# Half of the low weight parts made by an accumulating DMA

## The chip, the cores and the metric

The kernel runs on one core of a Trainium2 chip. The metric is the device time of one execution in microseconds (us).

## The reference

A trunk of two layers over 256 tokens with 2048 features, all in float32. Each of its four sub-layers ends in `x <- LayerNorm(ALPHA * x + sublayer(x))`.

```
layer 0: z = gelu(x @ w_in); u, v = split(z)                # 2048 -> 2 x 6144
         s = per-group 128 x 128 spatial weights (masked) on LayerNorm(v), + b_s
         (u * s) @ w_out                                    # 6144 -> 2048
layer 1: latent attention: q and kv latents of 512, 16 heads, rotary key of 64,
         chunk-causal softmax, output projection            # 2048 -> 2048
both:    h = causal width-3 depthwise conv(x @ w_up)        # 2048 -> 2 x 5504
         (silu(g) * a) @ w_down                             # 5504 -> 2048
```

With 256 tokens the weights are by far the largest data: every weight is read once and used for 256 tokens.

## The kernel before

**Float32 products in three parts.** A float32 value is written as the sum of a high part (rounded to the format that TensorE multiplies in one pass, `F32R` in the code) and a low part (value minus high part). A product is made of three: high x high, high x low and low x high. Activations are split as they arise. Weights are split chunk by chunk as they come from HBM.

**The chunks.** All weights are cut into 442 chunks of at most 128 x 2048 float32 (1 MB), numbered in the order of their use. 0 to 47 belong to stage `v`, 48 to 95 to stage `u`, 96 to 143 to `wo`, 144 to 229 to the up-projection of layer 0 (`up`), 230 to 272 to its down-projection (`dn`), 273 to 312 to the attention, 313 to 398 to the up-projection of layer 1, 399 to 441 to its down-projection.

**Feed.** The class `Feed` loads and splits them. `_load` takes a buffer `raw` and issues one plain DMA on SP's queue (L62). `_split` takes two more buffers, `wh` and `wl`, and for each half of the columns lets ACT copy the chunk into `wh`, which rounds it (L75), and DVE subtract `wh` from `raw` into `wl` (L76). `next(splits=2, loads=2)` hands out the next chunk, after it has put the splits of two chunks more, and the loads of two beyond those, into the streams. All of these buffers, together with the activations that live long, come from one pool of 22 buffers (`big`), so a load or a split waits until an earlier buffer is free.

**Order.** Each engine works through its own stream in order; the streams are laid down in about the order of the program, with splits moved ahead of evictions where the buffers allow it. ACT's stream thus mixes splits (L75) with evictions of finished products: in stage `u` and in the up-projection, `sum_halves` (L201 on ACT, L203 on DVE) and the convolution (L458 and following) for each group of four chunks. In these stages the weight is the stationary operand (`prod_a`): for every 128 x 128 block TensorE multiplies the high part with 512 columns (high and low part of the activation) and then the low part with 256 columns, so both parts of a chunk are needed within its first half microsecond. In the other stages the activation is stationary (`prod_b`), and each piece of 512 columns takes the high part twice and the low part once. All matmuls are issued by one helper and stand under L113.

**Layer boundaries.** `boundary` interleaves the last products of a sub-layer, its norm and the first products of the next one; there the splits of four chunks are asked for beforehand.

**GpSimd** sets a few constants at the start and one mask in stage `v` (L394), and issues no DMA.

Of the kernel before, what the change touches and what calls it, by code (L numbers as in the profile page):

```python
# [12 lines left out]
ALU = mybir.AluOpType  # L13
AX = mybir.AxisListType

P = 128
# [13 lines left out]
ALPHA = 4.0 ** 0.25  # L30
# [4 lines left out]

# columns of the per-partition constants
C_GMG = 0
# [5 lines left out]

# chunks at the end of a projection whose products are done block by block
SKEW = 3


class Feed:
    """The weight chunks in the order of their use: loaded ahead, and each split
    into a high and a low part whose sum is the float32 value."""  # L50

# [14 lines left out]
    def _split(self):  # L66
        i = self.split
        cols = self.chunks[i][1]
        raw = self.raw.pop(i)
        hi = self.pool.tile([P, 2048], F32R, tag="big", name=f"wh{i}")  # L70
        lo = self.pool.tile([P, 2048], F32R, tag="big", name=f"wl{i}")
        step = 512 if i == 0 else 1024 if cols == 2048 else cols // 2
        for o in range(0, cols, step):
            c = slice(o, o + step)
            self.nc.scalar.copy(hi[:, c], raw[:, c])  # L75
            self.nc.vector.tensor_tensor(lo[:, c], raw[:, c], hi[:, c].bitcast(F32), ALU.subtract)  # L76
        self.parts[i] = (hi, lo)
        self.split += 1
# [17 lines left out]
def trunk(ctx: ExitStack, tc: tile.TileContext, x, xT, gm_in, gm_wout, ffn_up, ffn_dn,  # L96
# [17 lines left out]

# [1 line left out]
    chunks = []  # L116
# [11 lines left out]

# [1 line left out]
    feed = Feed(nc, big, chunks)  # L130
    # products of zeros keep the array's clock up while the first loads are under way
    idle = cpool.tile([P, 512], BF16, name="idle")
# [5 lines left out]
    for j in range(4):  # L138
# [8 lines left out]
        for q in parts:  # L147
            hi = xhl[j][:, q, 0:S]
# [30 lines left out]

    # products whose stationary operand is the activation: [tokens, columns]  # L180
    def x_parts(xs, k, b):
# [3 lines left out]
    def prod_b(acc, parts, hi, lo, pieces, first, last):  # L185
        """acc: banks by piece; hi, lo: [P, columns]; pieces: (offset, width)"""
        xh, xl = parts
        for f, (o, w) in enumerate(pieces):
            mm(acc[f][:, :w], xh, hi[:, o : o + w], first, False)
            mm(acc[f][:, :w], xl, hi[:, o : o + w], False, False)  # L190
            mm(acc[f][:, :w], xh, lo[:, o : o + w], False, last)

    # products whose stationary operand is the weight: [features, 256 | 256]
    def prod_a(acc, xs, k, hi, lo, first, last):
# [11 lines left out]
    def split_act(src, name):  # L206
        """src: [P, 256] float32 -> high and low parts side by side"""
        t = tp.tile([P, 2 * S], F32R, tag="t2", name=name, bufs=6)
        nc.scalar.copy(t[:, 0:S], src)
        nc.vector.tensor_tensor(t[:, S : 2 * S], src, t[:, 0:S].bitcast(F32), ALU.subtract)  # L210
        return t
# [3 lines left out]
    def down(n_k, get_src, tag, ln, skew=SKEW):  # L215
        """[tokens, 2048] += src[k]^T w[k] with all eight banks; block 0 ends first"""
        acc = [[bank(f"{tag}_{b}_{f}") for f in range(4)] for b in range(2)]
        late = []
        a = {}
        for k in range(n_k):  # L220
            for j in range(k, min(k + 2, n_k)):
                if j not in a:
                    a[j] = split_act(get_src(j), f"{tag}a{j}")
            left = n_k - 1 - k
            hi, lo = feed.next(splits=2 if left > 8 else 3 if left > 3 else 4, loads=2 if left > 3 else 1)
            if left == 6:
                ln.prep()
            t = a.pop(k)
            if left < skew:
                late.append((t, hi, lo, k))  # L230
                continue
            for b in range(2):
                prod_b(acc[b], (t[:, b * P : (b + 1) * P], t[:, S + b * P : S + (b + 1) * P]),
                       hi, lo, full, k == 0, False)

        def end(b, f):
            for t, hi, lo, k in late:
                prod_b(acc[b][f : f + 1], (t[:, b * P : (b + 1) * P], t[:, S + b * P : S + (b + 1) * P]),
                       hi, lo, full[f : f + 1], False, k == n_k - 1)

        return acc, end

    def group(ln, tag):
        """the four chunks [4 k, 512 columns] after a norm, for block 0 and then for block 1"""
        parts = []
        acc = [bank(f"{tag}{b}") for b in range(2)]
        for b in range(2):
            for c in range(4):
                if b == 0:
                    parts.append(feed.next(splits=3 - c, loads=1))  # L250
                hi, lo = parts[c]
                for j in range(4):
                    k = 4 * c + j
                    prod_b([acc[b]], x_parts(ln.new, k, b), hi, lo, [(j * 512, 512)], k == 0, k == KD - 1)
                yield acc[b]

    def boundary(ln, acc, end, fs, tag, after):
        """the last products of a sub-layer, its norm, and the first products of the next one:
        each block's norm runs under the products of the other block"""
        for f in fs:  # L260
# [5 lines left out]
        if len(fs) == 2:  # L266
# [7 lines left out]
            g = group(ln, tag)  # L274
# [43 lines left out]
    class Norm:  # L318
        """LayerNorm(ALPHA * res + acc), in place of res; and its transpose in high and low parts"""

# [48 lines left out]

    # ================= layer 0: spatial-gating MLP =================  # L370
    halfp = [(0, 512), (512, 512)]
    v = []
    vst = st.tile([P, 2, 12, 6], F32, tag="vst", name="vst", bufs=1)
    for gi in range(6):
# [14 lines left out]
        if gi == 0:  # L389
            # spatial weights [j, g, i] with later chunks masked; sums over j and b_s on all partitions  # L390
            wT = slot([P, 2, 1024], "wT")
            wTg = wT[:, 0, :].rearrange("p (g i) -> p g i", g=NG)
            nc.sync.dma_start(wTg, w_sT)
            nc.gpsimd.memset(wTg[64:P, :, 0:64], 0.0)  # L394
            bsum = slot([P, 2, 1024], "bsum")
            nc.sync.dma_start(bsum[:, 1, :], b_s.to_broadcast([P, 1024]))
# [54 lines left out]

    # ================= gated MLP with the causal convolution =================
    def conv(layer, F, acc, name):
        """F: tile of the 86 up-projected feature tiles"""
        h = acc if acc.shape[-1] == S else sum_halves(acc, name)
# [56 lines left out]

    # ================= layer 1: latent attention =================
    cq = [slot([P, 4, 512], "cq", F32R)]
# [5 lines left out]
    def rope(dst, src, b, n, name):  # L520
        """dst, src: [P, n, 64]"""
        hf = ROPE // 2
# [11 lines left out]
    def latent(b, q, pieces):  # L534
        """RMS norm of a latent that lies in banks"""
        src = hqk[:, b, q * RANK : (q + 1) * RANK]
# [8 lines left out]
        o = 0  # L545
# [4 lines left out]
    def latent_put(b, q, dst, cg):  # L550
        """its transpose, in high and low parts"""
        src = hqk[:, b, q * RANK : (q + 1) * RANK]
# [47 lines left out]

    # rotary part of the queries: two chunks of [2 k, 1024]
    acc = [[bank(f"qr{b}_{f}") for f in range(2)] for b in range(2)]
# [20 lines left out]

    # head-major parts: four heads a chunk of [4 k, 512]
    def heads(dst, src, i, tag):
# [20 lines left out]
    def attend_a(h):  # L646
        """scores of head h and their softmax"""
        q, k = qT[h // 8][:, h % 8, :], kT[h // 8][:, h % 8, :]
# [5 lines left out]
        for b in range(2):  # L654
            nk = (b + 1) * P
            o = sc[:, cc[b]]
            # one accumulation bank for both blocks of queries
            mm(o, q[:, b * P : (b + 1) * P], k[:, :nk], b == 0, False)
            mm(o, qrT[r, h // 2, b * P : (b + 1) * P], krT[r, :nk], False, False)
            mm(o[:, nk - P : nk], negq, keyr, False, b == 1)  # L660
# [11 lines left out]
    def attend_b(h):  # L672
        """[keys of block 0, 256 queries | keys of block 1, 128 queries]"""
        p = probs[h]
# [34 lines left out]

    # output projection: two halves of the columns, the first one between the heads  # L710
    ln = Norm(2, res)
# [54 lines left out]
def _layout(inputs):  # L766
# [5 lines left out]
    def chunked(w, kk, width):  # L772
        """[K, N] -> [N / width * K / (128 kk), 128, kk * width]"""
        K, N = w.shape
        t = w.reshape(K // (P * kk), kk, P, N // width, width).transpose(3, 0, 2, 1, 4)
        return t.reshape(-1, P, kk * width)

    def pairs(w):
        """the up-projection: two tiles of a and two of g side by side"""
        n = (NF_FF // 2) * 2 * P  # L780
# [67 lines left out]
```

## Time and profile before

| | |
|---|---|
| time, median of 2 runs | 2565.43 us (2565.26 to 2565.59) |
| span of the profiled execution | 2564.7 us |
| TensorE matmuls | 2550.4 us busy, 99% |
| DVE | 1574.7 us, 61% |
| ACT | 1225.7 us, 48% |
| GpSimd | 2.4 us |
| DMA read from HBM | 476.00 MB, mean 186 GB/s over the span |

The profiled execution's span and the run times lie within a microsecond of each other, so durations of the trace can be set against the median directly. A row of a group or of the timeline names the line of the kernel, the engine, the operation and the tiles (output, arrow, inputs); in the timeline the first figure is the start, the second the duration, and the bracket at the end the idle time before it with what ended it. "PEclk" is the granted share of TensorE's full clock.

### The profile page before, as it was taken

The numbers are of one execution on the slowest core, as the hardware profiler recorded it, in microseconds if no ns is written. First come the engines' busy times: TensorE is split into PE (matmuls) and PEld (weight loads), VectorE is DVE, ScalarE is ACT, GpSimd is POOL, SyncE is SP. The second block draws the span as 40 slices with busy tenths as digits, with TensorE's granted clock in tenths as the row PEclk, the third lists the DMA queues.
The fourth block names the chain that finished last, engine by engine and source line by source line (L and its number), as shares of the span: only waits on it lengthen the run. The fifth ranks groups of instructions, "written<-read, shape, count | busy, mean of one in ns | idle before, by whom it ended". The sixth has DMA issues, their size and how long they took to land.

```text
span 2564.7 us, 32218 instructions
## 1 busy us (share of the span) xinstructions
PE 2550.4 (99%) x13041; PEld 2156.3 (84%) x13041; DVE 1574.7 (61%) x2284; ACT 1225.7 (48%) x1795; POOL 2.4 (0%) x15
## 2 busy tenths in 40 slices
PE   9999999999999999999999999999999999999998
PEld 7888888888888888888888888867888888888886
DVE  6444666675546766765675547745676576667554
ACT  6343444454443654654554434544365455446441
POOL 0000000000000000000000000000000000000000
PEclk9999999999999999999999999989999999999999
DMA  8555454466563645554565554423554454546552
GB/s 335 180 178 189 172 179 167 176 221 214 211 239 123 230 165 181 197 172 168 202 220 202 202 194 175 164 83 142 197 203 174 164 205 169 186 172 240 206 201 92
DMA packets 68837, 480.18 MB, mean 187 GB/s; under 512 B 7632, under 2 KB 8272, under 8 KB 11728
## 3 DMA queue, kind: packets, MB, share of 16 engines
q1 hardware_dynamic: 68688, 478.13, 52.1%
q8 instruction: 102, 1.67, 0.3%
q14 instruction: 47, 0.39, 0.0%
HBM read 476.00 MB, written 2.10 MB: 186 GB/s over the span
## 4 chain that ended last, share of the span: by engine, by line
PE 99%; DVE 1%; DMA 0%; SPq 0%; ACT 0%; issue 0%; DVEq 0%; ACTq 0%
PE up L113 36%; PE dn L113 18%; PE u L113 10%; PE wo L113 10%; PE v L113 10%; PE mo L113 4%; PE upf L113 2%; PE sc L113 2%; PE mkv L113 1%; PE qn L113 1%; PE kn L113 1%; PE vv L113 1%; PE mq L113 1%; PE s L113 1%; PE o L113 0%; PE qr L113 0%
## 5 line engine op out<-in xcount | busy, mean ns | idle before, releaser
L76 DVE TENSOR_TENSOR wl<-raw,wh 128x1024 fp32r<-128x1024 f32 (+2 forms) x886 | 1054.6, 1215 | 491.8 <-ACT wh L75 380.3
L75 ACT CAST wh<-raw 128x1024 fp32r<-128x1024 f32 (+2 forms) x886 | 890.7, 1044 | 567.7 <-DVE wl L76 242.0
L113 PE MATMUL up<-xhl,wh 128*128 128x512 f32 x2624 | 927.5, 399 | 0.0
L113 PE MATMUL up<-xhl,wl 128*128 128x256 f32 x2624 | 738.2, 281 | 0.0
L113 PEld LDWEIGHTS up<-xhl,wh 128*128 128x128 f32 x2624 | 493.8, 188 | 122.4
L113 PEld LDWEIGHTS up<-xhl,wl 128*128 128x128 f32 x2624 | 496.9, 189 | 0.1
L113 PE MATMUL u<-xhl,wh 128*128 128x512 f32 x768 | 268.8, 397 | 0.0
L113 PE MATMUL wo<-wh,woa 128*128 128x512 f32 x768 | 237.0, 390 | 0.0
L113 PE MATMUL v<-wh,xhl 128*128 128x512 f32 x768 | 235.5, 391 | 0.6 <-DVE xhl L150 0.3
L113 PE MATMUL u<-xhl,wl 128*128 128x256 f32 x768 | 212.5, 279 | 0.0
L113 PE MATMUL dn<-wh,dn0a 128*128 128x512 f32 x688 | 212.5, 390 | 0.0
L113 PE MATMUL dn<-wh,dn1a 128*128 128x512 f32 x688 | 211.8, 390 | 0.0
L113 PEld LDWEIGHTS v<-wh,xhl 128*128 128x128 f32 x768 | 144.2, 188 | 32.1 <-ACT wh L75 0.8
L113 PEld LDWEIGHTS u<-xhl,wh 128*128 128x128 f32 x768 | 143.5, 188 | 32.7
L113 PEld LDWEIGHTS wo<-wh,woa 128*128 128x128 f32 x768 | 144.1, 188 | 29.8
L113 PEld LDWEIGHTS dn<-wh,dn1a 128*128 128x128 f32 x688 | 129.2, 188 | 26.6
L113 PEld LDWEIGHTS dn<-wh,dn0a 128*128 128x128 f32 x688 | 129.1, 188 | 26.7
L113 PE MATMUL wo<-wl,woa 128*128 128x512 f32 x384 | 149.5, 390 | 0.0
L113 PE MATMUL v<-wl,xhl 128*128 128x512 f32 x384 | 147.3, 390 | 0.0
L113 PEld LDWEIGHTS u<-xhl,wl 128*128 128x128 f32 x768 | 144.8, 189 | 1.1
L113 PE MATMUL dn<-wl,dn0a 128*128 128x512 f32 x344 | 134.0, 390 | 0.0
L113 PE MATMUL dn<-wl,dn1a 128*128 128x512 f32 x344 | 134.0, 390 | 0.0
(204 smaller groups left out, 2147.8 us busy)
## 6 DMA issues: line engine op xcount, KB each, us to landing
raw<-in_ffn_up_dram SPq DMA_DIRECT2D x172, 1024.0 KB, 4.7
raw<-in_gm_in_dram SPq DMA_DIRECT2D x95, 1024.0 KB, 4.7
raw<-in_ffn_dn_dram SPq DMA_DIRECT2D x86, 1024.0 KB, 4.7
raw<-in_gm_wout_dram SPq DMA_DIRECT2D x48, 1024.0 KB, 4.7
raw<-in_ml_out_dram SPq DMA_DIRECT2D x16, 1024.0 KB, 4.7
raw<-in_ml_b_dram SPq DMA_DIRECT2D x14, 1024.0 KB, 4.8
raw<-in_ml_kv_dram SPq DMA_DIRECT2D x5, 864.0 KB, 4.8
lng<-in_ln_rows_dram SPq DMA_DIRECT2D x4, 1024.0 KB, 6.2
```

The costliest lines, as they stand in the source:

```text
L75: self.nc.scalar.copy(hi[:, c], raw[:, c])
L76: self.nc.vector.tensor_tensor(lo[:, c], raw[:, c], hi[:, c].bitcast(F32), ALU.subtract)
L113: nc.tensor.matmul(o, l, r, start=start, stop=stop, skip_group_check=True)
```

## The change

For odd chunks from number 5 on (219 of 442) DVE's subtraction goes. ACT writes minus the rounded chunk into `wl` (a multiplication by -1, in two halves), then GpSimd's queue issues one DMA that reads the chunk from HBM a second time and adds it to what stands in `wl`, and ACT makes the high part in two copies behind the multiplications. Even chunks and chunks 1 and 3 are split as before. The plain load of `raw`, the numbers of `next` and the pool stay as they are. The rest of the diff removes comments; line numbers behind `_split` are 12 higher in the changed kernel.

```diff
         hi = self.pool.tile([P, 2048], F32R, tag="big", name=f"wh{i}")
         lo = self.pool.tile([P, 2048], F32R, tag="big", name=f"wl{i}")
+        if i > 3 and i % 2:
+
+            for o in range(0, cols, 1024):
+                c = slice(o, min(o + 1024, cols))
+                self.nc.scalar.mul(lo[:, c], raw[:, c], -1.0)
+            self.nc.gpsimd.dma_start(lo[:, :cols], self.chunks[i][0][:, :cols], accum_op=ALU.add)
+            for o in range(0, cols, 1024):
+                c = slice(o, min(o + 1024, cols))
+                self.nc.scalar.copy(hi[:, c], raw[:, c])
+            self.parts[i] = (hi, lo)
+            self.split += 1
+            return
         step = 512 if i == 0 else 1024 if cols == 2048 else cols // 2
```

## The prediction

> **What bounds the kernel now.** I read the page first: busy shares, then the chain that ended last, then the groups.
>
> ```profile
> span 2564.7 us, 32218 instructions
> PE 2550.4 (99%) x13041; PEld 2156.3 (84%) x13041; DVE 1574.7 (61%) x2284; ACT 1225.7 (48%) x1795; POOL 2.4 (0%) x15
> PE 99%; DVE 1%; DMA 0%; SPq 0%; ACT 0%; issue 0%; DVEq 0%; ACTq 0%
> L76 DVE TENSOR_TENSOR wl<-raw,wh 128x1024 fp32r<-128x1024 f32 (+2 forms) x886 | 1054.6, 1215 | 491.8 <-ACT wh L75 380.3
> L75 ACT CAST wh<-raw 128x1024 fp32r<-128x1024 f32 (+2 forms) x886 | 890.7, 1044 | 567.7 <-DVE wl L76 242.0
> ```
>
> TensorE is the chain from end to end, and it is idle for 2564.7 - 2550.4 = 14.3 us of the span. DVE is far from a bound, so the subtractions (L76) that the change halves are under cover already. What matters is whether a weight chunk's low part is still ready when TensorE comes to it. I therefore looked for the places where it is ready with the least to spare, in the timeline.
>
> Nearly everywhere ACT runs far ahead of TensorE. But ACT works in order, and where its stream holds an eviction that must wait for a group of products, the splits behind it wait too. The tightest repeated place is in the up-projection, every fourth group. ACT's and TensorE's rows there:
>
> ```profile
> 1916.06 2.00 ACT L75 CAST wh<-raw 128x1024 fp32r<-128x1024 f32 x2 [0.77 <-DVE wl L76]
> ...
> 1946.21 0.37 ACT L201 COPY lo_1a<-up 128x256 f32<-128x256 f32 x1 [12.30 <-PE up L113]
> ...
> 1950.87 1.05 ACT L75 CAST wh<-raw 128x1024 fp32r<-128x1024 f32 x1
> 1951.82 0.60 ACT L458 ACTIVATE c_1a<-h_1a,cst 128x256 f32<-128x256 f32 x1
> 1952.32 0.36 ACT L201 COPY lo_1g<-up 128x256 f32<-128x256 f32 x1
> 1952.57 2.00 ACT L75 CAST wh<-raw 128x1024 fp32r<-128x1024 f32 x2
> ...
> 1958.61 0.28 PE L113 MATMUL up<-xhl,wl 128*128 128x256 f32 x1
> ```
>
> ACT stood idle for 12.30 us until group 4 of layer 1's up-projection (chunks 329 to 332) was done. Chunks 333 and 334 stand before the eviction in its stream (333 was cast at 1916.06, some 31 us ahead of its use); 335, odd, stands behind it. Its two halves were cast from 1950.87 to 1952.57 + 1.05 = 1953.6, and TensorE took its first low product at 1958.6. From the end of ACT's second half to the first use: **5.0 us of cover**. A DVE subtraction (1.2 us) fits into that; whether a DMA does is the question. In the changed kernel's instruction order the two multiplications by -1 of chunk 335 stand exactly where these two casts stand.
>
> The same reading at the other tight places of odd chunks:
>
> ```profile
> 858.10 1.99 ACT L75 CAST wh<-raw 128x1024 fp32r<-128x1024 f32 x2
> ...
> 864.75 0.28 PE L113 MATMUL up<-xhl,wl 128*128 128x256 f32 x1
> ...
> 945.92 2.00 ACT L75 CAST wh<-raw 128x1024 fp32r<-128x1024 f32 x2
> ...
> 955.21 0.28 PE L113 MATMUL up<-xhl,wl 128*128 128x256 f32 x1
> ...
> 300.14 2.01 ACT L75 CAST wh<-raw 128x1024 fp32r<-128x1024 f32 x2 [0.87 <-PE u L113]
> ...
> 311.38 0.27 PE L113 MATMUL u<-xhl,wl 128*128 128x256 f32 x1
> ...
> 2314.39 2.00 ACT L75 CAST wh<-raw 128x1024 fp32r<-128x1024 f32 x2
> ...
> 2320.65 0.39 PE L113 MATMUL dn<-wl,dn1a 128*128 128x512 f32 x1
> ```
>
> Chunk 151: 864.75 - 860.1 = 4.65 us, once. Chunk 167 (second half ends 945.92 + 1.04 = 946.96): 8.25 us; 183, 199, 215 and 231 lie the same way, so five. Chunk 55 (ends 302.15): 9.2 us, and five more of stage u, every eighth chunk. Chunk 399 (ends 2315.4): 5.2 us, once; 351, 367 and 383 repeat 335. So six odd chunks have about 5 us, five have 8.25, six have 9.2; a few others (5, 277, 279, 287, 321) lie between 6 and 10 and are left out of the sum.
>
> **The change, part by part.** It takes 219 odd chunks (5 to 441). Off DVE go 438 subtractions: 438 x 1.215 = 532 us of work, worth nothing, since the work that hid them is TensorE's own. On ACT come 438 multiplications. The trace has none; the nearest row is the cast of the same shape, 1.044 us: 438 x 1.04 = 457 us, which makes ACT 1683 of 2565 us (66%). By stage:
>
> ```profile
> 820.00:1070.00 250.00, 250.00 (x1397) 215.97 (x1396) 173.09 (x257) 133.57 (x201) 0.00 (x0) 1.00 0.52 186
> L394 POOL MEMSET wT<- 64x512 f32 x1 | 0.5, 525 | 40.9 <-DMA bsum<-in_b_s_dram 40.9
> ```
>
> In the up-projection 22 odd chunks in these 250 us add 46 us to 133.57, so 72%: no bound. Behind an odd chunk's multiplications on ACT stand the high part's copies and the next, even chunk, now 2 us later; that one is used a whole chunk later, and moves with the odd one's stall. GpSimd's queue gets 219 DMAs; only one memset (the L394 row) stands among them. SP's plain loads keep their order; their buffers come free from ACT's copy instead of DVE's subtraction, about when they did.
>
> The price is the accumulating DMA, from the end of the second multiplication to its landing; call it D. No row shows one. The nearest rows:
>
> ```profile
> 0.00:40.00 40.00, 38.07 (x156) 28.73 (x157) 28.61 (x32) 27.25 (x34) 1.86 (x14) 1.00 0.95 379
> q1 hardware_dynamic: 68688, 478.13, 52.1%
> raw<-in_ffn_up_dram SPq DMA_DIRECT2D x172, 1024.0 KB, 4.7
> lnb<-in_ln_rows_dram SPq DMA_DIRECT2D x4, 1024.0 KB, 8.4
> 1958.00:1965.00 7.00, 7.00 (x42) 6.07 (x41) 7.00 (x8) 5.52 (x6) 0.00 (x0) 1.00 0.77 287
> ```
>
> With the engines 0.95 busy they moved 379 GB/s, so about 399 at full: 1.049 MB is 2.63 us of all 16. A plain load lands after 4.7 us, hence 2.1 us beside the data. An accumulate reads the chunk again and the tile as well, and writes it; I take two passes, 5.3 us. Plain loads are in the way for 0.4 to 0.8 of the time there (0.77 in the row), so 0.6 x 2.63 = 1.6 us. GpSimd must write descriptors: between its 0.5 us for a memset and the 2.1 us above, I take 1.0. D = 2.1 + 5.3 + 1.6 + 1.0 = **10 us**. Bounds: 4.7, the plain load (one pass, nothing in the way), and 2.1 + 4 passes of 2.63 + one load of 2.63 + 2.1 = 17. The slowest row of this size, 8.4 us, lies nearer to 10 than to either end.
>
> The Trainium skill has a price for the add alone ("Collectives: The Full Stack", The bandwidth ceiling): it puts the loss in reading two sources, and measured about half of a copy's rate. That speaks against the change, and by it the sum would keep its two passes; no row of this trace shows an accumulate.
>
> Stall of TensorE at D = 10: six chunks at 5 us of cover lose 4 x 5.0 + 5.35 + 4.8 = 30.2; five lose 1.75 each, 8.8; six lose 0.8 each, 4.8. Together **44 us**.
>
> And a stall has a second price, which this trace shows:
>
> ```profile
> 1670.00:1675.00 5.00, 5.00 (x23) 4.08 (x23) 4.74 (x10) 4.45 (x8) 0.00 (x0) 1.00 0.43 177
> 1683.00:1690.00 7.00, 5.51 (x26) 3.95 (x24) 1.51 (x6) 2.93 (x9) 0.00 (x0) 0.87 0.45 152
> 1690.00:1700.00 10.00, 10.00 (x28) 5.86 (x28) 4.02 (x8) 5.70 (x11) 0.00 (x0) 0.50 0.00 0
> 1700.00:1705.00 5.00, 5.00 (x12) 3.81 (x13) 4.02 (x11) 0.91 (x4) 0.00 (x0) 0.50 0.00 0
> ```
>
> TensorE paused for 7.00 - 5.51 = 1.49 us, and the granted clock (the figure after POOL) then stood at 0.50 to 1705, some 17 us (0.13 of 7 us at double weight, 10, 5). In that time it made 28 matmuls in 10 us, where 23 in 5 us are made at 1.00: between 6.7 and 8.5 us lost, I take 7.5. If each pause of over 1.5 us does this, the six long ones cost 6 x 7.5 = 45; the five of 1.75 us are near the only pause seen, so I count half: 19. Together **64 us**.
>
> The Trainium skill ("TensorE: Matmul & The Clock Gate", Part 1: The HAM clock gate) says that the clock halves after an idle window of some 3.4 us and comes back after about as long of work. By that the six long pauses would cost 1.7 us each, 10 us in all, and the sum would be 2619. The row above shows a shorter pause and a longer loss; I go by the row.
>
> Sum: 2564.7 of the profiled execution + 44 + 64 = 2673; the median of the runs, 2565.4, is 0.7 above that span. **Forecast 2674 us**, 4.2% slower.
>
> **The rivals.** (A) *The DMA is hidden*, not slower. If D is at most 6.5 us, the worst pause is 6.5 - 4.65 = 1.85 and the six together lose 6 x 1.5 = 9, with no clock loss: 2574; at D = 5, nothing: 2566. For it: the plain load's 4.7 us. Against it: the accumulate has twice the bytes to read. It decides below 6.5 us.
> (B) *The DMA engines become the bound.* Plain traffic needs 478.13 / 399 = 1198 us; the accumulates move about 229 MB, 574 us a pass. Two passes: 2346 of 2565 us, not yet a bound. Three (both reads and the write one after the other): 2921 us; then the run-ahead is used up everywhere. It decides from (2565 - 1198) / 574 = 2.4 passes. For it: nothing here shows that reading the tile and writing it overlap. Against it: a plain load too reads and writes, in one pass.
> (C) *Pauses, but the clock holds*: 2565 + 44 = 2609 to 2619. For it: only one pause over 1.5 us is in the trace. Against: that one lost the clock.
> (G) *A gain* from the lighter DVE: no more than TensorE's idle 14.3 us, 2551. Against: none of that idle time repeats with the splits.
>
> **How the numbers follow.** Forecast (2630 to 2760, D of 8 to 13) 0.48, all slower; A 0.17, same; B 0.22, slower; C 0.10, half on each side of 2617; G 0.03, of which 0.01 faster by over 2%. 2% is 51 us, about what a measurement of this kernel can tell from no change. Faster 0.01, same 0.17 + 0.05 + 0.02 = 0.24, slower 0.48 + 0.22 + 0.05 = 0.75. The range: from 2572, which keeps A's upper half, to 2925, which keeps B at three passes and leaves four out.
>
> **What would show it.** In the changed profile: DVE near 1043 us, ACT near 1683; new waits of TensorE for the accumulating DMA, about 5 us long at chunks 151, 335, 351, 367, 383 and 399, and none where ACT runs ahead; behind each, a stretch of granted clock 0.5; the DMA issue row of the accumulate near 10 us to landing, and DMA share near 0.9. It is wrong if TensorE's idle time stays under 25 us (A), if the waits are spread evenly over all odd chunks with a DMA share near 1 (B), or if the pauses come without 0.5 behind them (C).

## The result and the profile after

The changed kernel takes 2731.53 us (2730.45 and 2732.61 in two runs) against 2565.43 us: a ratio of 1.066, with a 95% interval of 1.064 to 1.0681. It is slower by 166 us. The forecast was 2674 us with a range of 2572 to 2925.

From the page of the changed kernel: the span, the busy shares, the DMA queues (packets, MB, share of the 16 engines' time), the chain that ended last, and the DMA issues with the time from issue to landing.

```profile
span 2728.4 us, 32984 instructions
PE 2586.2 (95%) x13041; PEld 2179.4 (80%) x13041; DVE 1085.7 (40%) x1846; ACT 1618.9 (59%) x2233; POOL 192.1 (7%) x234
q1 hardware_dynamic: 68688, 478.13, 44.3%
q0 software_dynamic: 31536, 229.16, 42.9%
PE 64%; DMA 17%; issue 15%; ACT 3%; DVE 2%; POOL 0%; SPq 0%; POOLq 0%; DVEq 0%; ACTq 0%
raw<-in_ffn_up_dram SPq DMA_DIRECT2D x172, 1024.0 KB, 8.8
wl<-in_ffn_up_dram POOLq DMA_DIRECT2D x86, 1024.0 KB, 11.4
```

TensorE was 99% of the chain before; now DMAs (17%), time in which the engine waited for nothing that the profile shows ("issue", 15%), ACT and DVE hold over a third of it. Two differences give the whole loss. TensorE's idle time rose from 14.3 us to 2728.4 - 2586.2 = 142.2 us, by 127.9. Its busy time, for the same 13041 matmuls, rose from 2550.4 to 2586.2 us, by 35.8: matmuls at half clock take longer. By the trace's clock records half clock cost TensorE 43 us in the changed kernel and 8.5 us in the kernel before. Together 163.7 us, the difference of the two spans. DVE lost 489 us of work and that brought nothing.

The waits of TensorE in the changed kernel (total us, number, longest):

```profile
PE up L125 <- DMA wl<-in_ffn_up_dram: 40.8, 12, 5.9
PE lnt L376 <- DVE res L365: 25.2, 3, 15.2
PE dn L125 <- DMA wl<-in_ffn_dn_dram: 18.7, 5, 6.0
PE wo L125 <- ACT woa L221: 8.4, 2, 7.2
PE v L125 <- DMA wl<-in_gm_in_dram: 6.8, 4, 2.9
PE wo L125 <- DVE h_u L215: 5.6, 1, 5.6
PE qn L125 <- DMA wl<-in_ml_b_dram: 5.1, 1, 5.1
PE dn L125 <- ACT dn1a L221: 4.1, 1, 4.1
PE u L125 <- DMA wl<-in_gm_in_dram: 4.0, 4, 1.5
PE dn L125 <- ACT dn0a L221: 3.9, 1, 3.9
```

The rows that name the accumulating DMA (`wl`) hold 75 of the shown 123 us. The other 47 us (`lnt`, `woa`, `h_u`, `dn1a`, `dn0a`) name no accumulate: nearly all of them stand at the ends and starts of stages.

The place of the prediction's first example, chunk 335, in the timeline of ACT, GpSimd and TensorE:

```profile
2064.38 1.06 ACT L76 ACTIVATE wl<-raw 128x1024 fp32r<-128x1024 f32 x1
...
2066.08 1.07 ACT L76 ACTIVATE wl<-raw 128x1024 fp32r<-128x1024 f32 x1
...
2067.44 0.86 POOL L77 DMA_DIRECT2D wl<-in_ffn_up_dram  x1 [30.96 <-ACT wl L76]
...
2078.13 0.80 PE L125 MATMUL up<-xhl,wl 128*128 128x256 f32 x2 [5.85 <-DMA wl<-in_ffn_up_dram]
```

The multiplications end at 2067.15 and TensorE starts at 2078.13: D was 11.0 us here, and with 5.0 us of cover the pause is 5.85. What the pause does to the clock (the figure after POOL's), by stretch:

```profile
2072.00:2078.00 6.00, 0.28 (x2) 0.00 (x0) 2.69 (x4) 6.00 (x7) 0.86 (x1) 0.81 0.98 259
2078.00:2086.00 8.00, 7.87 (x34) 6.83 (x35) 0.84 (x1) 2.23 (x3) 0.86 (x1) 0.71 1.03 291
```

Half clock for 0.19 x 6 / 0.5 + 0.29 x 8 / 0.5 = 6.9 us, but the first 2.3 us of it fall into the pause itself. What remains, 4.6 us at half speed, costs 2.3 us.

### The profile page after: what moved, and what is told of

Same layout as the page of the kernel before. It is cut to its first block, busy times and chain, and to the rows that moved or that the text cites. A ratio compares the mean times of both kernels' runs of the same rounds, so it can differ in the third digit from the quotient of the medians.

```text
span 2728.4 us, 32984 instructions
## 1 busy us (share of the span) xinstructions
PE 2586.2 (95%) x13041; PEld 2179.4 (80%) x13041; DVE 1085.7 (40%) x1846; ACT 1618.9 (59%) x2233; POOL 192.1 (7%) x234
## 3 DMA queue, kind: packets, MB, share of 16 engines
q0 software_dynamic: 31536, 229.16, 42.9%
## 4 chain that ended last, share of the span: by engine, by line
PE 64%; DMA 17%; issue 15%; ACT 3%; DVE 2%; POOL 0%; SPq 0%; POOLq 0%; DVEq 0%; ACTq 0%
PE up L125 21%; PE dn L125 14%; PE wo L125 8%; PE u L125 7%; PE v L125 6%; DMA wl<-in_ffn_up_dram 4%; DMA raw<-in_ffn_up_dram 4%; DMA wl<-in_gm_in_dram 3%; PE mo L125 2%; DMA raw<-in_gm_in_dram 1%; PE sc L125 1%; DMA raw<-in_gm_wout_dram 1%; DMA raw<-in_ml_q_dram 1%; DMA wl<-in_ffn_dn_dram 1%; ACT wl L76 1%
## 5 line engine op out<-in xcount | busy, mean ns | idle before, releaser
L125 PE MATMUL up<-xhl,wl 128*128 128x256 f32 x2624 | 744.7, 284 | 40.8 <-DMA wl<-in_ffn_up_dram 40.8
L88 DVE TENSOR_TENSOR wl<-raw,wh 128x1024 fp32r<-128x1024 f32 (+2 forms) x448 | 532.6, 1211 | 551.2 <-ACT wh L87 524.5
L76 ACT ACTIVATE wl<-raw 128x1024 fp32r<-128x1024 f32 (+1 forms) x438 | 446.4, 1053 | 509.9 <-DMA raw<-in_ffn_dn_dram 118.5
L125 PEld LDWEIGHTS up<-xhl,wh 128*128 128x128 f32 x2624 | 501.2, 191 | 119.1
L125 PEld LDWEIGHTS up<-xhl,wl 128*128 128x128 f32 x2624 | 505.3, 193 | 45.3 <-DMA wl<-in_ffn_up_dram 45.2
L87 ACT CAST wh<-raw 128x1024 fp32r<-128x1024 f32 (+2 forms) x448 | 451.8, 1042 | 134.0 <-DMA raw<-in_ffn_dn_dram 36.6
L80 ACT CAST wh<-raw 128x1024 fp32r<-128x1024 f32 (+1 forms) x438 | 440.9, 1040 | 13.7 <-PE up L125 5.8
L125 PE MATMUL wo<-wh,woa 128*128 128x512 f32 x768 | 242.6, 397 | 14.7 <-ACT woa L221 8.4
## 6 DMA issues: line engine op xcount, KB each, us to landing
wl<-in_ffn_up_dram POOLq DMA_DIRECT2D x86, 1024.0 KB, 11.4
```

Of the source, the lines that this page charges most:

```text
L76: self.nc.scalar.mul(lo[:, c], raw[:, c], -1.0)
L125: nc.tensor.matmul(o, l, r, start=start, stop=stop, skip_group_check=True)
```

## The experiments

Theory T: TensorE waits for accumulating DMAs where their landing exceeds the cover, and at stage ends because the plain loads come late on crowded DMA engines. R1 blames ACT's additional work, R2 the DMA traffic wherever it stands. All ratios are against the kernel before on the same chip, with 95% intervals.

| kernel | accumulates | median us | ratio | TensorE idle us |
|---|---|---|---|---|
| the change | 219 | 2731.53 | 1.066 (1.064 to 1.0681) | 142.2 |
| no DMA, DVE adds | 0 | 2562.54 | 1.0001 (0.9989 to 1.0013) | 14.1 |
| i % 4 == 1 | 110 | 2595.45 | 1.0127 (1.0112 to 1.0142) | 38.8 |
| i % 4 == 3 | 109 | 2627.81 | 1.0251 (1.0235 to 1.0266) | 71.2 |
| tight chunks on DVE | 197 | 2657.61 | 1.0366 (1.035 to 1.0382) | 80.5 |
| stages thinned | 184 | 2657.27 | 1.0373 (1.0353 to 1.0394) | 88.2 |
| both of these | 164 | 2588.54 | 1.0116 (1.009 to 1.0142) | 33.5 |
| plain copies | 219 copies | 2578.5 | 1.0067 (1.0045 to 1.0089) | 29.0 |
| halves | 438 halves | 2671.54 | 1.0438 (1.0403 to 1.0473) | 100.7 |
| even chunks | 219 | 2748.44 | 1.072 (1.0691 to 1.0749) | 159.9 |

The idle times are the span minus TensorE's busy time on each page.

**The change without its DMA.**

```diff
-            self.nc.gpsimd.dma_start(lo[:, :cols], self.chunks[i][0][:, :cols], accum_op=ALU.add)
+            for o in range(0, cols, 1024):
+                c = slice(o, min(o + 1024, cols))
+                self.nc.vector.tensor_tensor(lo[:, c], lo[:, c].bitcast(F32), raw[:, c], ALU.add)
```

> The change with only its DMA taken away: ACT still multiplies by -1 and copies for odd chunks, and DVE adds the chunk to the low tile. Theory T (TensorE waits for accumulating DMAs that land after their cover is used up, and at stage ends for plain loads on crowded DMA engines): no pauses, 2566 us, within 5. Rival R1 (the 438 multiplications on ACT delay the splits and evictions behind them): most of the 166 us stays, over 2650. Rival R2 (the DMA traffic by itself, wherever the accumulates stand): 2566 too.

From its page:

```profile
PE 2549.5 (99%) x13041; PEld 2156.3 (84%) x13041; DVE 1578.7 (62%) x2284; ACT 1624.4 (63%) x2233; POOL 2.4 (0%) x15
```

ACT carries all of its 400 us more and the time is that of the kernel before, within some 0.1%. R1 falls: all of the loss comes with the DMA.

**Half the number, at two sets of places.**

```diff
-        if i > 3 and i % 2:
+        if i > 3 and i % 4 == 1:      # second kernel: == 3
```

> Accumulates only for chunks with i % 4 == 1 (110 instead of 219). Nearly none of the tight places (55, 151, 167, 335, 351, 367, 383, 399 and so on are all 3 modulo 4) is among them, and the engines are loaded 0.52 + 110 x 5.3 / 2565 = 0.75. T: 2566 to 2585. R1: half of the loss, 2648. R2: half of the loss, 2648.

> The same number and traffic, but for i % 4 == 3, which holds nearly all tight places. T: the pauses at 151, 335, 351, 367, 383, 399 (4 to 6 us each) and the short ones stay, those at the ends of wo and dn go: about 50 us of pauses and 25 of half clock, 2625 to 2650. R1 and R2: the same as with i % 4 == 1, since number and traffic are the same.

The software queue has the same share in both (23.3% and 23.0%), and one loses 1.3%, the other 2.5%, with intervals far apart. So place counts, not number and traffic alone: R2 by itself falls. The kernel with 1 modulo 4 lost 10 us more than T allowed: chunk 321 (4.1 us), 281 (3.4), 5 (3.0) and 385 (2.1), with 8 to 11.4 us of cover in the kernel before, are 1 modulo 4 too, and 7 us stay at starts and ends of stages (`h_u` 3.5, `lnt` 3.7). The waits of the other kernel:

```profile
PE up L125 <- DMA wl<-in_ffn_up_dram: 32.6, 9, 5.9
PE dn L125 <- DMA wl<-in_ffn_dn_dram: 10.2, 2, 6.2
PE qn L125 <- DMA wl<-in_ml_b_dram: 4.9, 1, 4.9
```

With half the traffic the pauses at the tight places are as long as before (351: 5.9; 383: 5.8; 399: 6.2), and no wait of the stage ends is left among its long ones. Its time lies in T's range, but TensorE was busy for 2555.6 us: that is 5 us more than before, where T had 25 of half clock, while its idle time rose by 57 where T had about 50.

**The tight chunks taken out.**

```diff
-        if i > 3 and i % 2:
+        if i > 3 and i % 2 and i not in TIGHT:
```

> The change, but 22 tight odd chunks (5, 55, 63, 71, 79, 87, 95, 151, 167, 183, 199, 215, 231, 277, 279, 287, 321, 335, 351, 367, 383, 399) are split as before; 197 accumulates stay. T: about 60 us of pauses and some 30 of half clock go, the pauses at stage ends stay: 2630 to 2650. R2: 197/219 of the loss stays, 2715. R1: the same, 2715.

TensorE's longest waits there:

```profile
PE lnt L379 <- DVE res L368: 22.7, 2, 14.3
PE dn L128 <- ACT dn0a L224: 10.1, 2, 6.6
PE up L128 <- DMA wl<-in_ffn_up_dram: 7.1, 6, 2.0
PE dn L128 <- DMA wl<-in_ffn_dn_dram: 7.1, 4, 3.5
PE wo L128 <- ACT woa L224: 5.4, 1, 5.4
```

22 of 219 accumulates carried 142.2 - 80.5 = 61.7 us of idle time, as T expected, and R2's 2715 is far off. But the half clock gave back only 2586.2 - 2575.6 = 10.6 us instead of some 30, so the time ended just above T's range; 7 us of it went with a pause of 1.5 us in the attention, behind which the clock fell in this kernel and not in the change. Of the waits that are left, 45 us stand at starts and ends of stages and 21 us are for accumulates at other chunks.

**The other half: thin the crowded stages, keep the tight chunks.**

```diff
+        thin = 96 <= i < 144 or 230 <= i < 277 or 399 <= i
-        if i > 3 and i % 2:
+        if i > 3 and i % 2 and not (thin and i % 4 == 3):
```

> The other half of the last cut: the tight chunks accumulate again, and only wo, both dn and the first chunks of the attention are thinned to i % 4 == 1 (185 accumulates). T: the pauses at the ends of wo, dn0 and dn1 go (some 55 us with 10 to 15 of half clock), those at 151, 335, 351, 367, 383 and at 287, 321 stay at 4 to 6 us, 399 and 231 go with the thinning: 2640 to 2670. If the stage ends hang on the tight chunks before them and not on the crowded engines, they stay: 2700 or more.

```profile
PE up L126 <- DMA wl<-in_ffn_up_dram: 38.8, 11, 6.1
...
PE lnt L377 <- DVE res L366: 2.1, 2, 1.3
```

The waits for the norm's transposes (`lnt`) fall from 25.2 to 2.1 us, the pauses for accumulates in the up-projection stay (38.8 of 40.8). The two cuts act on different waits. (184 accumulates are left; the expectation counted 185.) How crowded the engines are is seen in two stretches of the stage wo, 160 us from about its start and 38 us that end 5 us before its end, first of the changed kernel, then of the kernel with i % 4 == 3, which has half the accumulates (last two figures: DMA share, GB/s):

```profile
570.00:730.00 160.00, 154.41 (x680) 127.92 (x680) 50.34 (x72) 97.28 (x122) 12.96 (x15) 0.98 0.96 293
...
826.00:864.00 38.00, 20.51 (x76) 15.47 (x75) 15.56 (x24) 17.72 (x21) 2.59 (x3) 0.78 0.83 242
```

```profile
570.00:730.00 160.00, 160.00 (x707) 132.52 (x706) 71.73 (x85) 90.00 (x113) 6.91 (x8) 1.00 0.87 275
...
786.00:824.00 38.00, 38.00 (x169) 31.47 (x169) 17.05 (x24) 16.09 (x18) 1.73 (x2) 1.00 0.67 192
```

In the first stretch the changed kernel makes 680 instead of 707 matmuls; what it lacks went with the wait of 5.6 us at the stage's start (`h_u`) and the half clock behind it. The share of 0.96 shows later: at the stage's end TensorE is busy for only 20.5 of 38 us. The chain of waits runs through a plain load at the start of wo, at its end and at the end of layer 0's down-projection:

```profile
561.93 13.03 DMA raw<-in_gm_wout_dram
...
807.66 22.06 DMA raw<-in_gm_wout_dram
...
1586.43 20.51 DMA raw<-in_ml_q_dram
```

The load at the end of wo took 22 us from its issue, in a burst behind the norm's constants and the residual (5 MB issued within 3 us). The split that needs it stands in ACT's and DVE's streams ahead of the eviction and the norm, so TensorE waits for those. In the kernel with half the accumulates the run-ahead (from a load's landing to the first use of its chunk) grows from some 20 to some 45 us over wo, as in the kernel before; in the changed kernel it stays at 18 to 33. With the longer run-ahead the same five transfers go out over 13.4 us instead of 1.9, the last of them lands after 6.5 us, and TensorE does not wait.

**Both cuts.**

```diff
+        thin = 96 <= i < 144 or 230 <= i < 277 or 399 <= i
-        if i > 3 and i % 2:
+        if i > 3 and i % 2 and i not in TIGHT and not (thin and i % 4 == 3):
```

> The 22 tight chunks split as before, and in wo, in both dn and the first chunks of the attention only i % 4 == 1 accumulate, so that the DMA engines there have room (0.75 instead of over 0.95). T: pauses at the stage ends (34 us in the kernel without the tight chunks' accumulates at dn0's end and the next stage, 15 at wo's end, 9 at dn1's) go too; some short ones of 1 to 2 us stay: 2570 to 2595. If the stage ends are not made by crowded engines: 2640 to 2660 as with the tight chunks alone.

Within the range: 1.0116, 33.5 us of idle time. With 55 of the 219 accumulates given back, at places read from the two causes, 166 - 30 = 136 of the 166 us are gone; the rest are mostly short waits at further chunks.

**The addition by itself.**

```diff
-            self.nc.gpsimd.dma_start(lo[:, :cols], self.chunks[i][0][:, :cols], accum_op=ALU.add)
+            self.nc.gpsimd.dma_start(lo[:, :cols], self.chunks[i][0][:, :cols])
```

> The same DMAs on the same queue, but as plain copies into the low tile instead of additions (the low part is then the chunk itself). Everything that waits stays; only reading the tile and adding go. If the two passes of the sum are right, the software queue's share falls from 42.9% to 20 to 25%, the landing from 11.4 to about 8 us, the pauses at 335, 351, 367, 383 and 399 from 4.3 to 5.9 us to about 2, and the stage ends clear: 2585 to 2620. If the addition costs no pass of its own and the second 229 MB from HBM are the price: share and landing as in the change, 2700 to 2735.

This kernel leaves the addition out, so its output is not that of the reference; it serves for the time alone.

```profile
q1 hardware_dynamic: 68688, 478.13, 49.3%
q0 software_dynamic: 31536, 229.16, 24.8%
wl<-in_ffn_up_dram POOLq DMA_DIRECT2D x86, 1024.0 KB, 6.5
```

The same 229.16 MB from HBM, on the same queue and behind the same waits, take 0.248 x 2581.1 / 219 = 2.9 us of the 16 engines for a copy and 0.429 x 2728.4 / 219 = 5.3 us for an addition. The landing falls from 11.4 to 6.5 us, and time and landing are a little below what T expected; the pauses at 335, 351 and 383 fall to 1.7 to 2.3 us, and the stage ends clear. The second read from HBM is cheap; the additional time of the addition is what the change pays for. GpSimd too is busy for less, 0.53 us a DMA instead of 0.86. The trace counts the same packets and bytes for both kinds, so it does not show what the engines do in the 2.4 us more: that they are a second pass over the tile is an inference.

**Halves.**

```diff
                 self.nc.scalar.mul(lo[:, c], raw[:, c], -1.0)
-            self.nc.gpsimd.dma_start(lo[:, :cols], self.chunks[i][0][:, :cols], accum_op=ALU.add)
+                self.nc.gpsimd.dma_start(lo[:, c], self.chunks[i][0][:, c], accum_op=ALU.add)
```

> Each accumulate issued as two of half the columns, each right behind its own multiplication. In the up-projection TensorE needs the first half 2.8 us before the second, and the first half is issued 1 us earlier and has half the bytes. T: the pauses at 335, 351, 367, 383, 399 fall from 4.3 to 5.9 us to 1 to 3; the stage ends, which are waits for plain loads, stay: 2690 to 2715. If what counts is the bytes on the engines alone: 2730, no change.

```profile
PE lnt L376 <- DVE res L365: 27.0, 2, 15.6
PE up L125 <- DMA wl<-in_ffn_up_dram: 14.6, 10, 2.4
PE dn L125 <- DMA wl<-in_ffn_dn_dram: 8.2, 4, 3.0
```

As T has it, and better than its range: waits for accumulates in the up-projection fall from 40.8 to 14.6 us with the same bytes (45.4% of the engines' time), while the norm's wait at the stage ends stays (27.0). It is the latency of the first half, not the bytes, that the tight places pay.

**Even chunks.**

```diff
-        if i > 3 and i % 2:
+        if i > 3 and i % 2 == 0:
```

> Even chunks instead of odd ones: the same number and traffic, other places. In the trace of before the even chunks 166, 182, 198 and 214 had 5.0 us between ACT's second half and TensorE's first use, as 335 had. T: pauses of 5 to 6 us move to 166, 182, 198, 214 and to 320, and those at 335, 351, 367, 383, 399 go; stage ends stay: 2690 to 2740. If the pauses hang on the stage (layer 1's up-projection) or on the traffic there, they stay in layer 1.

TensorE at chunks 166 and 320:

```profile
1027.04 0.80 PE L125 MATMUL up<-xhl,wl 128*128 128x256 f32 x2 [5.21 <-DMA wl<-in_ffn_up_dram]
...
2035.42 1.22 PE L125 MATMUL up<-xhl,wl 128*128 128x256 f32 x4 [3.76 <-DMA wl<-in_ffn_up_dram]
```

The pauses moved as expected: 166, 182, 198 and 214 wait 4.5 to 5.6 us, 320 waits 3.8, and none of the odd tight chunks waits. The total lies a little over T's range; the waits at the stage ends got longer (30.4 us for the norm's transposes, against 25.2).

## Why the prediction was right, point by point

**Where the pauses come.** The cover read from the kernel before told the places: the six chunks with about 5 us paused for 3.8 to 5.9 us, 30.5 together against the 30.2 of the sum. The five with 8.25 us paused for 1.1, 1.6, 1.9, 3.6 and 6.0, together 14.2 against 8.8. Of the six in stage u, with 9.2 us, only three paused for 0.6 to 1.0. The five places left out of the sum lost 13 us, at chunks 5, 279, 287 and 321. Another 20 us fell on 13 chunks that the prediction did not name (3.5 us at 441, 3.2 at 219, 2.5 at 271). They had 11 to 28 us of cover in the kernel before and 5 to 14 in the changed one, where ACT's multiplications themselves wait for plain loads, and D was not one number: it ran from 7.7 to 16.3 us, with a median of 11.8. A cover read from the kernel before holds only as long as the loads come as early as there. The waits for accumulates come to 80 us in all, against the sum's 44.

**The size of D.** 11.0 us at chunk 335 against 10; the median landing in the up-projection is 11.4 us from issue. The 5.3 us taken for two passes are what the queue's share gives (5.3 us). GpSimd took 0.86 us for each issue where 1.0 was taken.

**What hid the rest.** ACT's 438 multiplications cost nothing, as the kernel without the DMA shows. DVE's relief was worth nothing as far as the runs show: the plain copies have it too and take 2578.5 us. DVE came to 1086 us and ACT to 1619, where 1043 and 1683 were said.

**The step that failed: rival B's capacity.** The sum compared 2346 us of DMA work with the whole span and found room. But a stage has its own account: in wo TensorE makes 707 matmuls in 160 us when nothing holds it, 5.43 us for the 24 of a chunk, so a pair of chunks gives the engines 10.9 us, and two loads and one accumulate need 2 x 2.63 + 5.3 = 10.6. The engines were at 0.96 there, the run-ahead did not build up, and the burst at the stage's end came late. The waits that name no accumulate come to 47 us, for which the prediction had no term; in 41 us of them, at the start and the end of wo and at the end of layer 0's down-projection, the chain runs through a plain load. At the very end of the kernel (`dn1a`) it runs through the last accumulate. B did not decide in the form it was given (three passes, waits at all odd chunks); its mechanism acted stage by stage with two.

**The clock: right in kind, too dear in size.** Half clock came behind most of the longer pauses, but the stretch behind the pause at 335 lasted 6.9 us with 2.3 us inside the pause, and cost 2.3 us instead of the 7.5 taken from the only pause seen before. The six long pauses cost 2.2 to 3.0 us each in this way, and all together TensorE's busy time rose by 35.8 us instead of 64. The rule of the Trainium skill ("TensorE: Matmul & The Clock Gate", Part 1: The HAM clock gate), which the prediction weighed and set aside, gives an estimate of 1.7 us a pause and was nearer for pauses in dense products. The 17 us of the kernel before belonged to the attention, where pause and surroundings differ: in the kernel without the DMA the same place again holds the clock at 0.50 for over 10 us after a pause of the same 1.48 us.

```profile
1685.00:1690.00 5.00, 3.52 (x20) 2.30 (x18) 1.65 (x7) 2.21 (x8) 0.00 (x0) 1.00 0.54 203
1690.00:1700.00 10.00, 10.00 (x26) 6.12 (x27) 5.06 (x10) 7.05 (x12) 0.00 (x0) 0.50 0.00 0
1700.00:1705.00 5.00, 5.00 (x17) 3.90 (x16) 2.87 (x9) 1.29 (x5) 0.00 (x0) 0.63 0.01 2
```

It does not come every time: in the changed kernel the pause at this place (1.49 us) is followed by no half clock. Whether the thinner products around it keep the clock down was not tried.

The term that was too large (64 for 35.8) made up for part of the two that were too small or missing (44 for 80, none for 47). That the sum, 108 us, came within 56 us of the measured 164 owes something to luck; the direction, the tight places and the price of an addition do not.

## What to carry to other kernels

Work that is taken off an engine with slack gains nothing, and what takes its place must fit the cover of the tightest place: read, for each prefetched operand, the time between its last writer's end and its first reader, and look where that is least, at evictions that hold back an in-order stream. Compare DMA demand with time stage by stage, not over the span: here a stage at a share of 0.96 did not build up its run-ahead, and one at 0.87 did. If an accumulate must be used, cut it into the pieces in which it is read, and leave the tight places to an engine.

## What the runs showed of the hardware

An accumulating DMA of 1 MB from HBM onto a tile takes 5.3 us of the 16 engines where a copy on the same queue takes 2.9, and lands 11.4 us after its issue instead of 6.5 in this kernel. In the changed kernel pauses of TensorE of 3.2 to 15 us cost their own length and mostly 1.4 to 3.2 us of half clock, in the trace's clock record in stretches of 3.4 us and multiples of it. Shorter pauses differ: of 1.5 to 2.9 us there, those at chunks 5, 51, 183 and 215 brought no half clock, but in the kernel without the tight chunks pauses of 1.6, 2.0 and 2.6 us brought 3.4 us of it each. A pause of 1.5 us in the attention was followed by 17 us at half clock in the kernel before, by 14 in the kernel without the DMA, and in the changed kernel, at the same place, by none.
